# Eleven shared landing semaphores and another cut of the last stores in a matmul with bias and residual

## The chip, the cores and the metric

The kernel runs on one core of one Trainium2 chip. The metric is the device time of one execution in microseconds (us), measured by the chip. A *landing* is the semaphore event with which one DMA engine reports its part of a transfer as done. One profiled execution of each kernel gives the page and the trace. The trace also holds, for each DMA packet, its start, duration and size, and for each semaphore event its time; where a number comes from these records and not from a printed view, the text says so.

## The reference

```python
def setup_inputs():
    batch, m, k, n = 16, 512, 1024, 768
    # x (16, 512, 1024), weight (1024, 768), bias (768), residual (16, 512, 768), all float32

def reference(x, weight, bias, residual):
    return (np.matmul(x, weight) + bias + residual).astype(np.float32)
```

The 8,192 rows are worked off as 64 tiles of 128 rows, numbered 0 to 63. A tile's result is 128 x 768 float32, so 3 KB in each of 128 partitions.

## The kernel before

The kernel records all operations in a list, works out which must wait for which, and then emits them with explicit semaphores. All transfers are issued from one queue (SyncE) in the order of a table. `('s', S, j0, j1)` stores tiles 16S + j0 to 16S + j1 - 1; numbers after that cut the store by rows (partitions). `('c', 3, 15, i)` stores the two column parts of the last tile.

```python
ORDER = [
 # ... loads and the stores of tiles 0 to 31
 ('r', 3, 7, 16), ('s', 2, 0, 16), ('s', 3, 0, 10), ('s', 3, 10, 11, 104), ('s', 3, 11, 13),
 ('s', 3, 13, 14), ('s', 3, 14, 15), ('c', 3, 15, 0), ('c', 3, 15, 1)]
# ...
edges = [0, *cut, P]
for p0, p1 in zip(edges, edges[1:]):
    dma(out_d[S, p0:p1, j0:j1, n0:n0 + nl],
        R[p0:p1, t0 % RR:t0 % RR + j1 - j0, n0:n0 + nl], rows(t0, t0 + j1 - j0, cs), [])
# ... in Program.emit: every transfer has a semaphore of its own
ins = emit(e)
if dma:
    sem = self.tc.alloc_semaphore(f"landed_{n}")
    mark[n] = (sem, 16)
    ins.then_inc(sem, 16)
```

At the end the program waits for all stores to land, passes barriers, clears its range of semaphores and passes a last barrier.

## Time and profile before

| | before |
|---|---|
| median of the first three executions | 210.88 us (210.81 to 211.23) |
| span of the profiled execution | 209.1 us |
| TensorE busy | 200.4 us, 96% |
| DMA queue, share of 16 engines | 97.7% |
| end of the last addition to the last landing (trace records) | 3.19 us |
| last landing to the end of the span (trace records) | 1.40 us |
| clearing of the semaphores | 287 ns |

TensorE sets the pace until the last matmul. What comes after the last addition is the tail of about 4.6 us (3.19 + 1.40): the last stores, the closing waits and barriers. The lines that show this stand in the prediction. Two more matter. The first is from the page (DMA queues: packets, MB, share of 16 engines), the second from the view of one source line (engine, operation, count: duration in ns as minimum, median and maximum; first and last start).

```profile
q1 hardware_dynamic: 4913, 87.05, 97.7%
...
L395 POOLq EVENT_SEMAPHORE_RANGE_CLEAR  x1: 287/287/287, 208.6 to 208.6; - x1
```

The 16 DMA engines are nearly saturated from beginning to end, so a delay of one engine may be carried along until the last store. And the clearing stands alone near the end of the span, where nothing hides it.

### The profile page before, as it was taken

The numbers are of one execution on the slowest core, as the hardware profiler recorded it, in microseconds if no ns is written. First come the engines' busy times: TensorE is split into PE (matmuls) and PEld (weight loads), VectorE is DVE, ScalarE is ACT, GpSimd is POOL, SyncE is SP. The second block draws the span as 40 slices with busy tenths as digits, with TensorE's granted clock in tenths as the row PEclk, the third lists the DMA queues.
The fourth block names the chain that finished last, engine by engine and source line by source line (L and its number), as shares of the span: only waits on it lengthen the run. The fifth ranks groups of instructions, "written<-read, shape, count | busy, mean of one in ns | idle before, by whom it ended". The sixth has DMA issues, their size and how long they took to land.

```text
span 209.1 us, 2471 instructions
## 1 busy us (share of the span) xinstructions
PE 200.4 (96%) x1273; PEld 80.9 (39%) x794; DVE 105.3 (50%) x141; ACT 66.1 (32%) x69; POOL 115.1 (55%) x71
## 2 busy tenths in 40 slices
PE   7899999999999999999999999999999999999990
PEld 2333433443443344344434433443443344344440
DVE  1458555445545544654455454645545544554451
ACT  2444513402640372310370093320091055330000
POOL 1100029759999805998039702999108950999000
PEclk9999999999999999999999999999999999999997
DMA  6999999999989999999999999999999999998994
GB/s 222 424 429 436 432 414 471 391 449 411 495 377 486 389 410 418 442 447 407 428 450 450 411 423 479 404 423 412 424 482 423 421 415 472 451 432 366 441 360 162
DMA packets 4924, 87.20 MB, mean 417 GB/s; under 512 B 557, under 2 KB 685, under 8 KB 1841
## 3 DMA queue, kind: packets, MB, share of 16 engines
q1 hardware_dynamic: 4913, 87.05, 97.7%
q8 instruction: 8, 0.13, 0.2%
q14 instruction: 3, 0.02, 0.0%
HBM read 61.88 MB, written 25.17 MB: 416 GB/s over the span
## 4 chain that ended last, share of the span: by engine, by line
PE 91%; DMA 4%; issue 1%; DVE 1%; SPq 0%; ACT 0%
PE psum_o L249 78%; PE pt L242 13%; DMA x_tile<-in_x_dram 4%; SPq L160 0%; DVE xt L218 0%; ACT xb L218 0%; DVE ro L221 0%; SPq L395 0%; SPq L363 0%
## 5 line engine op out<-in xcount | busy, mean ns | idle before, releaser
L249 PE MATMUL psum_o<-w_sb,xt 128*128 128x256 bf16 (+1 forms) x999 | 175.3, 324 | 1.8 <-DVE xt L218 0.5
L221 POOL TENSOR_TENSOR ro<-ro,bias_sb 128x768 f32<-128x768 f32 x50 | 88.8, 1811 | 46.8 <-DMA ro<-in_residual_dram 46.8
L218 ACT CAST xb<-x_tile 128x1024 bf16<-128x1024 f32 (+1 forms) x63 | 61.3, 1023 | 117.1 <-DMA x_tile<-in_x_dram 80.1
L260 PEld LDWEIGHTS <-xt 128*128 128x128 bf16 x520 | 50.9, 98 | 102.9 <-issue 101.0
L218 DVE COPY xt<-pt 128x1024 bf16<-128x1024 bf16 x64 | 44.1, 691 | 83.6 <-PE pt L242 83.6
L221 DVE TENSOR_TENSOR ro<-psum_o,ro 128x768 f32<-128x768 f32 (+2 forms) x51 | 47.6, 934 | 6.3 <-POOL ro L221 4.3
L242 PE MATMUL pt<-ident,xb 128*128 128x128 f32 x256 | 38.3, 273 | 0.5 <-DVE xb L218 0.3
L221 POOL TENSOR_TENSOR ro<-ro 128x768 f32<-128x768 f32 x14 | 24.9, 1813 | 25.0 <-DMA ro<-in_residual_dram 25.0
L242 PEld LDWEIGHTS pt<-ident,xb 128*128 128x128 f32 x256 | 29.7, 140 | 15.5 <-issue 12.3
L221 DVE TENSOR_TENSOR ro<-psum_o,bias_sb 128x768 f32<-128x768 f32 x14 | 13.2, 948 | 0.0
L304 PE MATMUL psum_o<-warm 128*128 128x512 bf16 x18 | 6.4, 514 | 1.4 <-DVE warm_a L224 1.4
L218 DVE CAST xb<-x_tile 128x512 bf16<-128x512 f32 (+1 forms) x4 | 1.9, 492 | 6.1 <-DMA x_tile<-in_x_dram 6.1
L218 ACT CAST w_sb<-ro 128x768 bf16<-128x768 f32 x4 | 3.3, 832 | 3.7 <-DMA ro<-in_weight_dram 3.7
L218 POOL CAST w_sb<-ro 128x768 bf16<-128x768 f32 x1 | 0.8, 824 | 5.9 <-DMA ro<-in_weight_dram 5.9
L304 PEld LDWEIGHTS psum_o<-warm 128*128 128x128 bf16 x18 | 2.2, 126 | 4.6 <-issue 2.9
L218 DVE CAST w_sb<-ro 128x768 bf16<-128x768 f32 x3 | 1.7, 557 | 2.0 <-DMA ro<-in_weight_dram 2.0
L218 ACT ACT_TABLE_LOAD x1 | 1.3, 1283 | 0.9 <-SPq L363 0.9
L321 DVE STREAM_SHUFFLE bias_sb<-bias_row 128x768 f32<-128x768 f32 x1 | 1.0, 1024 | 0.0
L224 DVE MEMSET warm<- 128x256 uint32 x1 | 0.3, 272 | 1.1 <-SPq L363 1.1
L224 DVE MEMSET bias_row<- 128x768 f32 x1 | 0.7, 698 | 0.2 <-issue 0.2
L224 POOL MEMSET ident<- 128x128 f32 x1 | 0.2, 204 | 0.5 <-SPq L363 0.5
L312 POOL TENSOR_SCALAR_AFFINE_SELECT ident<-ident 128x128 f32<-128x128 f32 x1 | 0.3, 293 | 0.2 <-POOL ident L224 0.2
(7 smaller groups left out, 0.7 us busy)
## 6 DMA issues: line engine op xcount, KB each, us to landing
out_dram<-ro SPq DMA_DIRECT2D x3, 6144.0 KB, 34.4
x_tile<-in_x_dram SPq DMA_DIRECT2D x3, 5120.0 KB, 24.5
ro<-in_residual_dram SPq DMA_DIRECT2D x3, 3840.0 KB, 32.1
x_tile<-in_x_dram SPq DMA_DIRECT2D x3, 3072.0 KB, 39.8
ro<-in_residual_dram SPq DMA_DIRECT2D x3, 2304.0 KB, 18.5
x_tile<-in_x_dram SPq DMA_DIRECT2D x4, 1024.0 KB, 10.9
x_tile<-in_x_dram SPq DMA_DIRECT2D x2, 2048.0 KB, 23.4
out_dram<-ro SPq DMA_DIRECT2D x1, 3840.0 KB, 13.1
```

Of the source, the lines that this page charges most:

```text
L218: op(eng, lambda e: (e.copy if eng == "act" else e.tensor_copy)(out=dst, in_=src), rd, wr)
L221: op(eng, lambda e: e.tensor_add(out=dst, in0=a, in1=b), rd, wr)
L224: op(eng, lambda e: e.memset(dst, v), [], [wr])
L242: op("pe", lambda e, q=q: e.transpose(out=pt[:, q, :], in_=words[:, ts(q, P)], identity=ident), [("XB", t % XB_N, 2 * q // n_q), "ident"], ...
L249: return e.add_instruction(mybir.InstMatmult(name=nc.get_next_instruction_name(), ins=[e.lower_ap(rhs), e.lower_ap(lhsT, for_matmul_weight ...
L260: op("pe", lambda g: g.ldweights(lhsT), rd)
L304: op("pe", lambda e: e.matmul(PO[i][:, 0:512], lhsT=warm[:, 0:P], rhs=warm, start=True, stop=True), ["warm"], [("PO", i)])
L312: op("pool", lambda e: e.affine_select(out=ident, in_=ident, compare_op=mybir.AluOpType.not_equal, fill=1.0, base=0, pattern=[[-1, P]], ch ...
L321: op("dve", lambda e: e.stream_shuffle(out=bias_sb, in_=bias_row, mask=[0] * QUAD), ["bias_row"], ["bias"])
```

## The change

The intent is to clear fewer semaphores, and to give the DMA engines that are late at the end fewer rows of the last stores. A semaphore is used again only for a transfer issued when the queue already knows that the last transfer on it has landed, so no wait is added.

```diff
- ('r', 3, 7, 16), ('s', 2, 0, 16), ('s', 3, 0, 10), ('s', 3, 10, 11, 104), ('s', 3, 11, 13),
- ('s', 3, 13, 14), ('s', 3, 14, 15), ('c', 3, 15, 0), ('c', 3, 15, 1)]
+ ('r', 3, 7, 16), ('s', 2, 0, 16), ('s', 3, 0, 10), ('s', 3, 10, 12, 96, 116),
+ ('s', 3, 12, 14), ('s', 3, 14, 15), ('c', 3, 15, 0), ('c', 3, 15, 1)]
...
+            if dma:
+                free = [i for i, used in enumerate(slots) if seen.get(used[-1], -1) >= 0]
+                if not free:
+                    free = [len(slots)]
+                    slots.append([])
+                slot[n] = free[0], len(slots[free[0]]) + 1
+                slots[free[0]].append(n)
...
+        landings = [self.tc.alloc_semaphore(f"landed_{i}") for i in range(len(slots))]
...
             if dma:
-                sem = self.tc.alloc_semaphore(f"landed_{n}")
-                mark[n] = (sem, 16)
-                ins.then_inc(sem, 16)
+                i, k = slot[n]
+                mark[n] = (landings[i], 16 * k)
+                ins.then_inc(landings[i], 16)
```

More of the change, by code (lines that the diff above doesn't have):

```diff
@@ L65, in emit @@
         ops, known = self.ops, {e: {} for e in self.engines}
-        lane, count, snap, waits = [], {}, [], []
+        lane, count, snap, waits, slots, slot = [], {}, [], [], [], {}
         for n, (eng, _, deps, dma) in enumerate(ops):
```

## The prediction

> **What bounds the kernel now.** I read the page's chain that ended last first, because it tells which engine a change must shorten.
>
> ```profile
> PE 91%; DMA 4%; issue 1%; DVE 1%; SPq 0%; ACT 0%
> PE 200.4 (96%) x1273; PEld 80.9 (39%) x794; DVE 105.3 (50%) x141; ACT 66.1 (32%) x69; POOL 115.1 (55%) x71
> ```
>
> TensorE is the bound: it works in 96% of the span and makes up 91% of the chain. The change touches no instruction of TensorE, VectorE, ScalarE or GpSimd: the order of instructions on these engines is the same in both programs apart from source lines. So whatever it does must come after the last matmul. Next I read the timeline from 200 us.
>
> ```profile
> 201.22 2.59 PEld L260 LDWEIGHTS <-xt 128*128 128x128 bf16 x16 [0.23 <-issue]
> 203.33 1.23 DVE L221 TENSOR_TENSOR ro<-psum_o,ro 128x512 f32<-128x512 f32 x2 [0.84 <-PE psum_o L249]
> 204.05 1.13 SPq L160 DMA_DIRECT2D out_dram<-ro  x2
> ```
>
> The last addition ends at 203.33 + 1.23 = 204.56 us, the last store is issued right after it (until 204.05 + 1.13 = 205.18), and the span ends at 209.1. So 4.5 us follow the last arithmetic, and this tail is the only place to win. The windows view cut finely over it (after the stretch: its length, then busy time of PE, PEld, DVE, ACT and POOL, then TensorE clock, DMA share, GB/s) shows how the stores run out:
>
> ```profile
> 205.00:205.50 0.50, 0.00 (x0) 0.00 (x0) 0.00 (x0) 0.00 (x0) 0.00 (x0) 1.00 1.01 391
> 205.50:206.00 0.50, 0.00 (x0) 0.00 (x0) 0.00 (x0) 0.00 (x0) 0.00 (x0) 1.00 0.87 320
> 206.20:206.40 0.20, 0.00 (x0) 0.00 (x0) 0.00 (x0) 0.00 (x0) 0.00 (x0) 1.00 0.41 149
> 206.40:206.60 0.20, 0.00 (x0) 0.00 (x0) 0.00 (x0) 0.00 (x0) 0.00 (x0) 1.00 0.25 87
> 206.80:207.00 0.20, 0.00 (x0) 0.00 (x0) 0.00 (x0) 0.00 (x0) 0.00 (x0) 0.75 0.10 36
> 207.20:207.40 0.20, 0.00 (x0) 0.00 (x0) 0.00 (x0) 0.00 (x0) 0.00 (x0) 0.50 0.06 20
> ```
>
> DMA share times 16 is the number of DMA engines still moving: 16 until 205.5, 4 at 206.5, one (0.06 x 16) at 207.3. The program waits for one straggling DMA engine. The semaphore records of the trace agree: the sixteen landings of the last store run from 206.37 to 207.74 us, and the last is 0.51 us behind the one before. After 207.74 come 1.4 us of closing waits, barriers and semaphore clearing.
>
> To see why one engine is late I sorted the 4,913 packet records of the trace into sixteen chains: a packet follows the packet of the same engine that ended about 3 ns before it. This is my reconstruction, no view prints it. The chains' last packets end at 207.41, 206.89, 206.60, 206.52, 206.46, 206.41, 206.34, 206.23, and eight between 206.04 and 206.20. The lateness comes from instruction fetches, of which the page's queue list shows eight:
>
> ```profile
> q8 instruction: 8, 0.13, 0.2%
> ```
>
> Each is 16 KB and holds one DMA engine for about 1 us (931 to 1,100 ns in the packet records), and the fetches went to different chains; the last at 191.7 us. The late chains are those with a fetch.
>
> **What the Trainium skill says.** The page "Runtime: NRT & Kernel Launch", section "Instruction fetch mechanics", says that the sequencer drives its own DMA queue to fetch 16 KiB blocks and calls the cost mostly hidden. The trace agrees on the size; the cost shows again as a DMA engine that is 1 us behind. "DMA: Bandwidth & Descriptors", section "Why a DMA increments its semaphore by 16 and not by 1", says that a transfer issued from this queue uses the largest k up to 16 that divides its outermost dimension, on the lowest-numbered k engines, and that the sequencer adds the other 16 - k at once. The trace agrees: the 104-row store leaves 14 semaphore events (13 engines and the sequencer), the 24-row one 13 (12 and the sequencer). The same section warns that two transfers in flight on one semaphore can satisfy each other's wait. The new code gives a semaphore again only when the queue already knows its previous transfer landed, so no wait is added and none becomes unsafe; no run of before shows sharing.
>
> **The change part by part.**
>
> (1) Eleven shared landing semaphores for 36. The transfers are 36 in both programs, and the built programs show the same waits. What shrinks is the range cleared at the end: from 46 semaphores to 21. In the trace this is one GpSimd instruction of 287 ns between two barriers, so on the path. If its time goes with the count, 287 x 21/46 = 131 ns, a gain of 0.16 us; if it is fixed, nothing. I count 0.1.
>
> (2) The cuts move bytes between DMA engines. Count rows of 3 KB per engine for tiles 58 and 59 together. Before: tile 58 as 104 rows on 13 engines (8 each) and 24 on 12 (2 each), tile 59 inside a 128-row store (8 each). That is 18 rows on engines 0 to 11, 16 on engine 12, 8 on engines 13 to 15. After: 96 rows on 16 engines, 20 on 10, 12 on 12, i.e. 6, 2 and 1 rows of two tiles each: 18 on engines 0 to 9, 14 on 10 and 11, 12 on 12 to 15. So engines 0 to 9 have the same bytes, 10 to 12 four rows less, 13 to 15 four more. A 3,072-byte packet takes 121 ns (packet records), so four rows are 0.48 us.
>
> Which chain is which engine? Those that skipped the 104-row store are 13 to 15, the one that skipped only the 24-row one is 12: its end is 206.60, theirs 206.04, 206.14, 206.19. Fetches hit the chain ending 206.89 (at 23.9 us), then 12, then two of 13 to 15 (at 71.5 and 95.9), then four others, the last the one ending 207.41. If fetches go round in order, the chain of 206.89 is 11; and a round of eight, 7 to 14, would make the last one 10. I take that, with about 70% belief: then both worst stragglers lose four rows. The one of 207.41 also lost about 0.5 us to slow packets inside its pieces of tile 58 (its ten rows took 1.74 us instead of 1.2), which may or may not return.
>
> New ends: 10: 207.41 - 0.48 = 206.93 with the slow packets, 206.4 without; 11: 206.41; 12: 206.12; 13 to 15: at most 206.19 + 0.48 = 206.67, less where they idled at the end anyway; the rest up to 206.52 unchanged. So the last packet moves from 207.41 to between 206.5 and 206.95, a gain of 0.45 to 0.9; I take 0.65.
>
> (3) The stores stand differently in time. Tiles 58 and 59 go at about 194.4 instead of 191.4 and 197.5; the 3.84 MB store ahead of them runs until 199 to 201, so this is hidden. Tiles 60 and 61 go together when 61 is done, at 200.5 where 61 went alone, and first packets follow some 1.1 us after an issue (last store: 204.58 to 205.68), so at 201.6. Early engines then run dry from about 201 to 201.6, late ones do not; and the early ones already wait for the last two stores. Cost 0. Two-tile rows of 6 KB take 234 ns against 2 x 121 = 242: nine of them, below 0.1 us.
>
> Sum: 0.65 + 0.1 = 0.75 us: 210.88 - 0.75 = about 210.15.
>
> **The rivals.** A: the straggler is one of engines 0 to 9. It keeps its 18 rows, and only the clearing remains: 210.7 to 210.9. For it: ten of the twelve engines that it could be are there; against it, the order of the fetches. B: the mechanism holds and the slow packets were an effect of the narrow cuts; the last engine is then a middle one at 206.5, and with 0.16 for clearing the time is about 209.8. C: a new transfer turns up as a bound: tiles 60 and 61 start later, engines run dry, and the tail grows by up to the wait of 0.6 us: 211.2. Against it: engines that run dry are those with slack of 0.2 to 1.3 us. D: three small stores cost issue time. An issue took 1.93 us at 191.8 in the trace, in the middle of a fetch (191.66 to 192.59); the three now fall at 194.4, where no fetch runs, and 6 us remain before the next issue. Nothing.
>
> **Range and chances.** My weights are 65% for the sum (209.9 to 210.4), 15% for A, 12% for B, 8% for C. That gives 209.8 to 210.7 for 8 in 10. Two per cent is 4.2 us, almost the whole tail of 4.5 us, which no rebalancing of stores removes; a loss of that size would need a new wait in the TensorE stage, of which the programs show none. So same 0.98.
>
> **What would show it.** Right: TensorE's work, its chain and the fetches unchanged within 0.1 us; DMA share above 0.06 ends near 206.9 instead of 207.4; the sixteen landings of the last store spread over 0.5 to 0.9 us instead of 1.37; the clearing instruction near 130 to 190 ns. Wrong: one engine still moving at 207.3 (rival A), a clearing of 287 ns, or a DMA share well below 1 between 202 and 205 with the last landing later (rival C). A later first matmul or any pause of TensorE would upset the whole argument.

## The result and the profile after

| | before | after |
|---|---|---|
| median of six executions | 210.68 us (210.48 to 211.23) | 210.25 us (210.03 to 210.56) |
| ratio of the fast runs | | 0.9976 (95% interval 0.9961 to 0.9991) |
| last addition to last landing | 3.19 us | 2.78 us |
| last landing to end | 1.40 us | 1.24 us |
| clearing | 287 ns | 157 ns |

A ratio here is the mean time of one kernel's fast runs over the mean of the other's fast runs of the same rounds, so it is not quite the ratio of the medians. The change is a gain of about 0.43 us by the medians, clear of the noise but far inside 2%.

The chain and the busy times of the page after, to be held against the first fence of the prediction:

```profile
PE 92%; DMA 4%; issue 1%; DVE 1%; SPq 0%; ACT 0%
PE 200.3 (96%) x1273; PEld 80.7 (39%) x794; DVE 105.3 (50%) x141; ACT 66.1 (32%) x69; POOL 115.2 (55%) x71
```

Nothing moved there. The timeline after, for the end of the arithmetic:

```profile
200.71 4.40 SPq L168 DMA_DIRECT2D out_dram<-ro  x4
...
203.53 1.23 DVE L229 TENSOR_TENSOR ro<-psum_o,ro 128x512 f32<-128x512 f32 x2 [0.84 <-PE psum_o L257]
```

The last addition ends at 204.76 us, 0.2 us later than before. That is no effect of the change: in the traces it ends between 204.45 and 204.86 us, in both groups of kernels. So from here on I count the tail from the last addition. The fine windows of the tail after (columns as in the prediction):

```profile
205.50:206.00 0.50, 0.00 (x0) 0.00 (x0) 0.00 (x0) 0.00 (x0) 0.00 (x0) 1.00 0.94 352
206.20:206.40 0.20, 0.00 (x0) 0.00 (x0) 0.00 (x0) 0.00 (x0) 0.00 (x0) 1.00 0.51 184
206.40:206.60 0.20, 0.00 (x0) 0.00 (x0) 0.00 (x0) 0.00 (x0) 0.00 (x0) 1.00 0.43 159
206.60:206.80 0.20, 0.00 (x0) 0.00 (x0) 0.00 (x0) 0.00 (x0) 0.00 (x0) 1.00 0.39 143
206.80:207.00 0.20, 0.00 (x0) 0.00 (x0) 0.00 (x0) 0.00 (x0) 0.00 (x0) 1.00 0.21 72
207.00:207.20 0.20, 0.00 (x0) 0.00 (x0) 0.00 (x0) 0.00 (x0) 0.00 (x0) 1.00 0.12 41
207.20:207.40 0.20, 0.00 (x0) 0.00 (x0) 0.00 (x0) 0.00 (x0) 0.00 (x0) 1.00 0.00 0
```

The picture of before was one engine working alone at the end. Now six engines are still at work at 206.7 (0.39 x 16) and two at 207.1: the lone straggler is gone, but a group of late engines is still there. The landings of the last store run from 206.41 to 207.54 us, a spread of 1.13 us. Of the clearing:

```profile
L403 POOLq EVENT_SEMAPHORE_RANGE_CLEAR  x1: 157/157/157, 208.3 to 208.3; - x1
```

### The profile page after: what moved, and what is told of

Read it like the earlier page. It is cut to its first block, busy times and chain, and to the rows that moved or that the text cites. A ratio compares the mean times of both kernels' runs of the same rounds, so it can differ in the third digit from the quotient of the medians.

```text
span 208.8 us, 2471 instructions
## 1 busy us (share of the span) xinstructions
PE 200.3 (96%) x1273; PEld 80.7 (39%) x794; DVE 105.3 (50%) x141; ACT 66.1 (32%) x69; POOL 115.2 (55%) x71
## 4 chain that ended last, share of the span: by engine, by line
PE 92%; DMA 4%; issue 1%; DVE 1%; SPq 0%; ACT 0%
PE psum_o L257 79%; PE pt L250 13%; DMA x_tile<-in_x_dram 4%; SPq L168 0%; DVE xt L226 0%; ACT xb L226 0%; DVE ro L229 0%; SPq L403 0%; SPq L371 0%
```

## The experiments

Theory going in: 0.13 to 0.16 us come from the clearing, and the rest from rows taken off the late DMA engines. Rivals: the late engines are not the relieved ones; or the slow packets in the old cut, not the number of rows, made the straggler. The runs went to three jobs, the first on one chip and the other two on another, each with its own runs of the kernel before (medians 210.85, 210.97 and 210.66 us). All were correct.

### The two parts alone

Shared semaphores alone: the table's stores as before.

```diff
- ('s', 3, 10, 12, 96, 116), ('s', 3, 12, 14), ('s', 3, 14, 15), ...
+ ('s', 3, 10, 11, 104), ('s', 3, 11, 13), ('s', 3, 13, 14), ('s', 3, 14, 15), ...
```

> The eleven shared semaphores alone, stores cut as in the kernel before. My theory: only the clearing instruction shrinks, from 287 ns to about 157 ns, since it covers 21 semaphores as in the changed kernel; the spread of the last store's landings stays that of before (1.37 us, one engine about 0.5 us behind the next), and the time falls by 0.1 to 0.15 us (ratio 0.9994). Rival: sharing itself changes the transfers or their issue (the time falls by 0.4 us as in the full change, or the landing spread shrinks).

Measured: median 210.28 us, but 210.11 to 211.23 over six executions; ratio 0.9987 (0.9968 to 1.0005). The median fell by 0.57 us, not by 0.1 to 0.15, but the interval is wide and includes no change. In its profile the clearing took 157 ns and the end after the last landing 1.24 us, as expected. The tail before it was shorter than expected: 2.52 us from the last addition to the last landing, with no lone straggler. So the same cut gave 3.19 us in one trace and 2.52 us in the other. The rival, that sharing itself removes the straggler, does not hold: the padded kernel below shares as well and has it again (3.11 us). The straggler comes and goes.

New cuts alone: one semaphore for each transfer again.

```diff
-                i, k = slot[n]
-                mark[n] = (landings[i], 16 * k)
-                ins.then_inc(landings[i], 16)
+                sem = self.tc.alloc_semaphore(f"landed_{n}")
+                mark[n] = (sem, 16)
+                ins.then_inc(sem, 16)
```

> The new cuts alone, one semaphore for each transfer. My theory: the clearing stays at 287 ns, the landings of the last store spread over about 1.1 us as in the changed kernel, the time falls by 0.3 us (ratio 0.9986). Rival: the cuts are worth nothing and the whole gain was semaphores and chance: ratio 1.000 and a last landing no earlier than in the kernel before, counted from the end of the last addition.

Measured: median 211.29 us (210.22 to 211.96), ratio 1.0031 (1.0009 to 1.0053). Clearing and closing were back at 288 ns and 1.40 us. The time missed both expectations: four of the six executions took 211.26 us or more, above the median of before in this job (210.85). The profiled one was the fastest (2.58 us from last addition to last landing), so it does not tell where the others lost their time.

### The cut taken away

```diff
- ('s', 3, 10, 12, 96, 116),
+ ('s', 3, 10, 12),
```

> The changed kernel with tiles 58 and 59 in one store of 128 rows, not cut. If relieving engines 10 to 15 is what the change wins, its time rises by the rows it gives back: four rows of 0.12 us on the stragglers, so 0.2 to 0.5 us above the changed kernel. If the stragglers are among engines 0 to 9 (rival A), an uncut store takes two rows of 3 KB away from those (16 in place of 18), and the time falls by about 0.2 us below the changed kernel.

Measured: median 210.08 us, all five executions between 210.00 and 210.32; ratio 0.9972 (0.9956 to 0.9988). The relief of engines 10 to 15 is gone, and nothing is lost. Its tail in the same windows:

```profile
206.20:206.40 0.20, 0.00 (x0) 0.00 (x0) 0.00 (x0) 0.00 (x0) 0.00 (x0) 1.00 0.45 154
206.40:206.60 0.20, 0.00 (x0) 0.00 (x0) 0.00 (x0) 0.00 (x0) 0.00 (x0) 1.00 0.25 87
206.60:206.80 0.20, 0.00 (x0) 0.00 (x0) 0.00 (x0) 0.00 (x0) 0.00 (x0) 1.00 0.07 21
206.80:207.00 0.20, 0.00 (x0) 0.00 (x0) 0.00 (x0) 0.00 (x0) 0.00 (x0) 1.00 0.00 0
```

The last landing, at 207.06 us, is about 0.5 us earlier than in the changed kernel's profile (207.54), with the last addition at 204.79 us (204.76 there).

The packet records show what the cut costs. A packet of 6 KB takes 234 ns and one of 3 KB 121 ns when nothing disturbs it. I counted the packets that begin after 198.5 us and take over 1.3 times that, and summed their excess:

| kernel | cut of tile 58 or 58 and 59 | slowed packets | excess in sum |
|---|---|---|---|
| before | 104, 24 | 15 | 3.0 us |
| shared semaphores alone | 104, 24 | 11 | 2.4 us |
| shared and padded (below) | 104, 24 | 14 | 2.4 us |
| changed | 96, 20, 12 | 8 | 3.6 us |
| changed, second and third time | 96, 20, 12 | 15 and 9 | 3.8 and 2.4 us |
| new cuts alone, twice | 96, 20, 12 | 12 and 14 | 3.1 and 2.9 us |
| probe (below) | 96, 20, 12 | 15 | 3.0 us |
| halves (below) | 64, 64 | 12 | 2.6 us |
| uncut, three kernels in four traces | none | 0 | 0 |

Single packets took up to 1,307 ns in place of 234. The coarse windows show the same thing as bytes for the busy time. This view counts a packet, its bytes and its whole duration, in the window in which it starts (checked on the packet records); so in windows this short the share is not how busy the engines were, but share and bytes belong to the same packets. First the changed kernel, then the uncut one, 200 to 201 us:

```profile
200.00:201.00 1.00, 1.00 (x8) 0.29 (x3) 0.69 (x1) 0.00 (x0) 0.00 (x0) 1.00 0.75 246
```

```profile
200.00:201.00 1.00, 1.00 (x8) 0.29 (x3) 0.72 (x1) 0.00 (x0) 0.00 (x0) 1.00 0.59 246
```

Both start packets of 246 GB/s, the cut kernel's with a share of 0.75, the uncut one's with 0.59. The difference, 0.16 us on each of 16 engines or 2.6 us, is the excess of the slowed packets that start there (2.7 us in the packet records).

Two limits of this table. The probe's sixteen pieces of 15 rows and fewer, sent near 177 us, have none: their 128 packets took at most 131 ns. And slow packets are not confined to cut stores: near 77 us transfers of 128 rows have them too, in the uncut kernel as well (packets of 30 KB of up to 1,587 ns in place of 1,138).

### Which engines are late

A probe sends tile 32 in pieces of 15, 14, 13 and so on down to 1 row and then 8. By the rule for the number of engines that the prediction quotes, each piece uses one engine fewer than the one before, so the landing that is missing tells which engine is which.

```diff
- ('s', 2, 0, 16),
+ ('s', 2, 0, 1, 15, 29, 42, 54, 65, 75, 84, 92, 99, 105, 110, 114, 117, 119, 120), ('s', 2, 1, 16),
```

> A probe, not a faster kernel: the first tile of the third store is sent in sixteen pieces of 15, 14, 13 and so on down to 1 row and then 8 rows, so that each piece uses one DMA engine fewer than the piece before. Where a piece's landings lack one that the piece before had, that is the engine of the next lower number. If engines 7 to 14 are those that the instruction fetches held, the engines that drop out first (14, 13, 12, 11, 10) land about 1 us later than engines 0 to 3. If rival A holds, the late ones are among the low numbers. The time should be 0 to 1 us above the changed kernel.

Measured: one look, 210.86 us, state unknown. The semaphore records have 15 engine landings for the first piece, 14 for the second and so on to one, as the rule wants. Reading off which landing drops out: in the load just before the pieces, which landed between 175.88 and 178.17 us, engines 0, 7, 8, 10 and 15 were early (by 176.1 us), 1, 2 and 4 in the middle (176.6 to 176.8), and 3, 5, 6, 9, 11, 12, 13 and 14 late (177.2 us and after), 11 the latest. So my round of 7 to 14 is wrong: 7 and 8 are early, 3, 5 and 6 are late. Engines 11 to 14 are late as I had assumed. This is one execution, read after seven of the eight fetches.

For the changed kernel's own profile the records of its pieces say more. The three latest landings of the 96-row store (202.99, 203.11 and 203.15 us) come again in the 20-row store, which only engines 0 to 9 serve, 0.46, 0.45 and 0.43 us later (203.45, 203.56, 203.58), which is the time of two packets of 234 ns. So the three latest engines were among those that kept their 18 rows. In its second and third profile the latest were not: the two latest landings of the third (202.95, 203.03) have no successor in the 20-row store, whose last landing is 203.00, too early by 0.4 us. In those two profiles the last addition to last landing took 2.28 and 2.39 us, in the first 2.78.

### Sharing, clearing and the spread of the executions

The second job asked whether one semaphore a transfer makes slow executions. The changed kernel again, without edit:

> The changed kernel once more, beside the others of this job. In the runs so far the kernels with shared semaphores (the changed one, the shared ones alone, the uncut one) had one execution of 17 above 210.6 us, those with one semaphore a transfer 15 of 23. If that is not chance, all or nearly all executions here lie between 210.0 and 210.6 us. If it is chance, about half lie above.

Measured: median 210.24 us (210.08 to 210.85), ratio 0.9976 (0.9958 to 0.9994). Five of the six are within 210.0 to 210.6.

The uncut store with one semaphore a transfer (the uncut kernel with the edit of the new cuts alone):

> The uncut store of tiles 58 and 59 with one semaphore a transfer, so the uncut kernel with the sharing taken back. If sharing is worth the clearing alone: 0.13 to 0.16 us above the uncut kernel's 210.08, so 210.25 and steady. If one semaphore a transfer brings slow executions, its median is 210.6 to 211.3 with a spread of about 1 us. If instead the narrow cuts bring them, it is steady near 210.25.

Measured: median 210.23 us, all six executions between 210.19 and 210.31; ratio 0.9972 (0.9956 to 0.9988). So many semaphores do not by themselves bring slow executions, and sharing is worth about the clearing alone here, as the first expectation said. The clearing took 269 ns for 44 semaphores.

Shared semaphores, the old cut, and 25 semaphores that nothing uses:

```diff
+        self.unused = [self.tc.alloc_semaphore(f"unused_{i}") for i in range(25)]
```

> The shared semaphores alone (stores cut as in the kernel before), with 25 semaphores allocated that nothing uses, so that the clearing covers 46 again. The clearing instruction should return to 287 ns and the end after the last landing to 1.40 us. If slow executions come with the number of semaphores that transfers add to, this stays steady at 210.4; if they come with the clearing or the number allocated, it spreads to 211.2 like the kernel before.

Measured: median 210.71 us (210.62 to 210.92), ratio 0.9994 (0.9976 to 1.0012). The clearing was 288 ns and the closing 1.40 us again. The time fits neither expectation: steady, but 0.3 us above 210.4, and 0.43 us above the same stores without the padding (210.28, in another job and on another chip), of which the clearing explains 0.16. Its profile caught the straggler of before once more, 3.11 us from last addition to last landing:

```profile
206.40:206.60 0.20, 0.00 (x0) 0.00 (x0) 0.00 (x0) 0.00 (x0) 0.00 (x0) 1.00 0.26 92
206.60:206.80 0.20, 0.00 (x0) 0.00 (x0) 0.00 (x0) 0.00 (x0) 0.00 (x0) 1.00 0.20 72
206.80:207.00 0.20, 0.00 (x0) 0.00 (x0) 0.00 (x0) 0.00 (x0) 0.00 (x0) 1.00 0.10 36
207.00:207.20 0.20, 0.00 (x0) 0.00 (x0) 0.00 (x0) 0.00 (x0) 0.00 (x0) 1.00 0.07 26
207.20:207.40 0.20, 0.00 (x0) 0.00 (x0) 0.00 (x0) 0.00 (x0) 0.00 (x0) 1.00 0.05 15
```

The same sorting of packets into chains as in the prediction tells why. The chain that ends last (207.37) finished the store ahead of it at 200.47, in the middle of the field, and then took 1.90 us for its eight rows of tile 58 where undisturbed chains took 0.95. Without that it would have ended near 206.4. A fetch alone did not make it last; slowed packets of the 104-row piece did.

The new cuts alone a second time:

> The new cuts with one semaphore a transfer once more, for a profile of an execution above 211 us, which five of its six runs were; the profiled one was the sixth. If the time is lost to one DMA engine at the end, the last landing comes 0.5 us or more after the one before it and over 3.0 us after the last addition (2.58 in the fast one), with the last addition still at 204.4 to 204.8. If it is lost earlier, the last addition itself ends near 205.5.

Measured: one look, state unknown, 210.39 us, 2.53 us from last addition to last landing. It did not catch a slow execution. (The expectation miscounts: four of the six earlier runs were above 211 us, not five.)

### What in the cut slows the packets, and the last comparison

Two halves of 64 rows: no bytes move between engines, and all sixteen engines serve both.

```diff
- ('s', 3, 10, 12, 96, 116),
+ ('s', 3, 10, 12, 64),
```

> Tiles 58 and 59 in two stores of 64 rows: all sixteen DMA engines in both, four rows each, so no bytes move between engines. In the traces so far every kernel with a cut store has packets of these stores slowed to between 300 and 1,300 ns (234 is usual for 6 KB), 3 to 4 us in sum over the engines, and the uncut ones have none. If the slowing comes from a store that uses fewer engines, there is none here. If it comes from any store of fewer than 128 rows (its rows then lie otherwise on the engines than in a store of 128), the slowed packets are here too, 2 to 4 us in sum, and the median is 0.1 to 0.4 us above the uncut kernel.

Measured: median 210.33 us (210.20 to 210.86), ratio 0.9984 (0.9971 to 0.9998). Slowed packets: 12, 2.6 us in sum. So it is not the smaller number of engines. The time, though, is only 0.04 us above the uncut kernel of the same rounds (210.29, below), less than the 0.1 to 0.4 us expected. Each cut tried here also sends the rows of the same tiles in two or three transfers one after another; whether the number of rows or this division slows the packets, no run separates.

The grouping of before, uncut:

```diff
- ('s', 3, 10, 12, 96, 116), ('s', 3, 12, 14), ('s', 3, 14, 15), ...
+ ('s', 3, 10, 11), ('s', 3, 11, 13), ('s', 3, 13, 14), ('s', 3, 14, 15), ...
```

> Shared semaphores with the stores grouped as in the kernel before (58 alone, 59 with 60, 61 alone), the store of tile 58 uncut. If the cut is what cost the kernel before its slow executions and the grouping is indifferent, this is as steady and as fast as the uncut kernel: 210.0 to 210.4, no slowed packets. If the grouping of the change matters, it is 0.2 us or more above it.

Measured: median 210.15 us (209.82 to 210.31), ratio 0.9970 (0.9957 to 0.9982), no slowed packets. The last line of its profile that shows a DMA engine at work, and the line after it:

```profile
206.20:206.40 0.20, 0.00 (x0) 0.00 (x0) 0.00 (x0) 0.00 (x0) 0.00 (x0) 1.00 0.25 82
206.40:206.60 0.20, 0.00 (x0) 0.00 (x0) 0.00 (x0) 0.00 (x0) 0.00 (x0) 1.00 0.00 0
```

All engines end within 0.65 us of one another (landings of the last store 206.16 to 206.80) without any cut. This execution's last addition ended at 204.45, so it is 2.35 us from there.

The uncut kernel and the changed kernel, again without edit, in the same rounds:

> The uncut kernel again, beside the changed kernel on the same chip: it has shared semaphores and the new grouping, no cut. Expected: 210.0 to 210.35 in every execution, median 0.1 to 0.2 us below the changed kernel's, whose executions spread wider (210.05 to 210.85 so far).

> The changed kernel for the third time, for the comparison with the uncut kernel in the same rounds: median 210.25, some execution above 210.4; slowed packets of 3 to 4 us in sum in its profile.

Measured: uncut 210.29 us (210.09 to 210.41), ratio 0.9976 (0.9962 to 0.9989); changed 210.31 us (210.05 to 210.41), ratio 0.9977 (0.9964 to 0.9989). There is no difference between the two here, against my expectation of 0.1 to 0.2 us (two of the uncut executions also lay above the 210.35 expected, and the changed kernel's slowed packets, 2.4 us in sum, were fewer than expected). So the new cuts gain nothing over no cut, to within the intervals. The version with shared semaphores, the old grouping and no cut has the lowest median of this job, 210.15 us; its interval overlaps with that of the changed kernel, so it beats the kernel before, and at most matches or slightly beats the changed one.

All profiles together, from the last addition to the last landing:

| cut | traces, us | mean |
|---|---|---|
| 104, 24 | 3.19, 3.11, 2.52 | 2.94 |
| 96, 20, 12 | 2.78, 2.28, 2.39, 2.58, 2.53 | 2.51 |
| none | 2.27, 2.41, 2.35, 2.57 | 2.40 |

(The probe and the halves, 2.97 and 2.60, are left out.)

## Why the prediction was right or wrong

**The number.** 210.15 us was forecast, 0.73 below the 210.88 of before; the measured median is 210.25, and 0.43 below the kernel before of the same six-run count. The time lies in the range; the gain was put too high by 0.3 us. Of the signs named beforehand, TensorE's work and the clearing (157 ns) came out; the landings of the last store spread over 1.13 us, not 0.5 to 0.9, and the last packet ended at 207.20 us with the addition 0.2 us later, so near 207.0 and not between 206.5 and 206.95. That the number held is in part luck, as the next points show.

**Where to look** was right. TensorE's line changed by 0.1 us, and everything happened after the last addition.

**The semaphores** (part 1) were right, and a little better than counted. The clearing fell by 130 ns against 156 by proportion, and the drain ahead of it from 117 to 88 ns, so the stretch after the last landing fell from 1.40 to 1.24 us, in every trace with 21 semaphores. I had counted 0.1 us.

**The cuts** (part 2) had the arithmetic of rows right and the reason wrong. The term of 0.65 us measured 0.41 us between the two first profiles (3.19 to 2.78), and 0.43 us between the means of the table; the medians, 0.43 us less 0.16 for the clearing, leave 0.27. The step that failed is "Which chain is which engine?", with its belief of 70% that "both worst stragglers lose four rows". The probe showed other late engines than the round of 7 to 14, and in the changed kernel's first profile the three latest were among engines 0 to 9, as rival A has it. That the late chains are those with a fetch, on which this step builds, was not shown either: the prediction itself gives two of engines 13 to 15, which end early (with ten rows fewer), a fetch. The relief reached the late engines only in some executions. What went instead was the term that I left open, that the slow packets "may or may not return". They were the larger part of the straggler: 0.95 us in the padded kernel's profile, about 0.5 us in that of before. After 198.5 us they come with every cut of the last stores that was tried and with none of the uncut ones. The old cut's cost is shown most directly by the kernel with the old grouping and tile 58 uncut: 0.51 us below before in the same rounds, of which 0.16 is the clearing. The new cuts have them too, in equal sum, but in none of their five traces (the probe aside) does the last engine look slowed: the last landing of the 96-row store came 1.37 to 1.39 us after the last of the store ahead, the time of six packets of 234 ns. Why the new cut spares the late engines and the old one did not in two of its three traces, I have not shown; with so few traces it may be chance.

**Rival B** said that the slow packets were an effect of the narrow cuts and would be gone after. Half of that held: they are an effect of the cuts, of the new ones too, and so they did not go. Without cuts they go, and the time is 210.08 to 210.29, not the 209.8 of B.

**The timing of the stores** (part 3) and rival C: counted by overlap in the packet records, the sixteen engines were fully busy from 200 to 201 us in every trace (0.98 to 1.02; over 1 because the packets of one engine overlap by about 3 ns, where the prediction reads a gap of 3 ns). From 201 to 202 the changed kernel has 0.94 to 0.97 in its three traces and the uncut kernels with the new grouping 0.86 to 0.92, against 1.02 before and 1.02 with the old grouping uncut. So some engines did run dry where the prediction put it, and no cost shows: from last addition to last landing the new grouping uncut took 2.27 to 2.57 us, the old one 2.35. The grouping made no measurable difference either (210.15 against 210.29, with overlapping intervals). Rival D: the second and third small store took 1.26 and 1.23 us to issue with no fetch under way, so the fetch explains at most the rest of the 1.93 us, but there was time for them.

**Left open.** The two parts do not add up: alone they gave 0.9987 and 1.0031, together 0.9976. The new cuts with one semaphore a transfer ran above 211.2 us in four of six executions of one job, and no trace caught one of those; the same program gave 210.39 in a later single look. Since the uncut store with as many semaphores was steady, the count of semaphores alone is not it. Over all executions the two seem to act together. I count as late what lies above 210.6 us, or above 210.76 where 44 or 46 semaphores are cleared (0.16 us longer): with cut stores and 46 semaphores 24 of 50 are late, with cut stores and 21 semaphores 3 of 28, with uncut stores none of 21. No run shows why, and the groups are spread over jobs and chips. How the rows of a store of fewer than 128 rows lie on the engines, and what two engines then share, no run measured.

## What to carry to other kernels

When all DMA engines are saturated, look at how the landings of the last store spread before trimming it, and ask of a lone late engine whether its own packets were slow before you give it less work. A store cut by rows to balance engines can disturb its own balance, as the old cut did here: try the uncut one beside it, and run each often enough to see the spread of its executions as well as its median. Semaphores that are cleared at the end cost about 5 ns each, in the open.

## What the Trainium skill lacked or had wrong

- "DMA: Bandwidth & Descriptors", section "Why a DMA increments its semaphore by 16 and not by 1": the rule for the number of engines held for every piece here (15 down to 1 in the probe). The page gives the layout of rows on engines for 128 partitions only, and no duration of single packets of smaller stores beside others. Here: 8 to 15 slowed packets with 2.4 to 3.8 us of excess in each of ten traces with stores of 12 to 104 rows at the end, and none after 198.5 us in four traces with stores of 128 rows only.
- "DMA: Bandwidth & Descriptors", section "Rules for kernel authors": it advises against two transfers to disjoint partition halves because they serialize. The advice holds here (210.33 against 210.29 us uncut); the row does not mention the slowed packets (2.6 us in sum). Whether the halves serialize, no run looked at.
- "Runtime: NRT & Kernel Launch", section "Instruction fetch mechanics": the fetch is called mostly hidden. For TensorE that agrees (busy 200.4 of 209.1 us). But each fetch holds one DMA engine for 0.9 to 1.1 us, and in the trace of before the packet that starts as a fetch ends took 0.4 to 0.55 us longer than others of its size, after all eight fetches (1,379 to 1,461 ns for 24 KB in place of 912). What that costs at the end of the kernel, no run isolates.
- No page gives the duration of the instruction with which the kernel itself clears a range of semaphores at its end: 157 ns for 21, 225 ns for 35, 269 ns for 44 and 287 ns for 46.
